# Second-block projections in products of 512 columns

## The chip, the cores and the metric

The kernel runs on one core of a Trainium2 chip. The metric is the device time of one execution in microseconds; the time given is the median of the runs.

## The reference, cut to what matters

Two transformer blocks follow one another on 512 tokens of width 1024 (fp32). The first is a hybrid mixer (differential attention and a convolution), cross-attention and a convolutional feed-forward. The second, in which the change lies, is this:

```
h = rms_norm(x);  proj = h @ w_in                     # 1024 -> 9232
sb_qkv, gdn_qkv, gdn_z, gdn_b, gdn_a, gate_sb, gate_gdn = split(proj)
o_sb  = stick_breaking_attention(q, k, v)             # 8 heads of 128
gq, gk, gv = silu(causal_depthwise_conv(gdn_qkv))     # kernel of 4
o_gdn = rms_norm(gated_delta_rule_chunked(l2(gq), l2(gk), gv, g, beta)) * silu(z)   # 8 heads of 128
x = x + (sigmoid(gate_sb) * (o_sb @ w_branch_sb) + sigmoid(gate_gdn) * (o_gdn @ w_branch_gdn)) @ w_out
x = x + peer_ffn(rms_norm(x))                         # product-key experts
```

## The kernel before, in words

Every matrix product of fp32 values is made of three: an operand is split into a high and a low part, and `mm3` (L198) adds high by high, low of the moving operand by high of the weights, and high by low, all into one bank of PSUM. A weight chunk of 128 x 2048 comes by two DMAs into the tiles `wraw` (three buffers), and `load_w` (L204) splits it: ScalarE copies the high part `wh`, VectorE subtracts for `wl` (L194, L195). The activations lie transposed as `yh` and `yl`: 8 tiles of 128 features by 512 tokens.

The second block (`block2`, L791) runs several strands at once. `gdn_in` (L1093) loops over eight heads h. For each it projects one chunk for query and key (`w_gqk`) and one for value and z (`w_gvz`) by `proj_tr` (L308), whose two banks are given by a rotation of tags (`ROT`, L33): p, gd and sz for head 0, p alone from head 1 on; p has two banks. The emptied banks go through a convolution and silu on ScalarE, VectorE and GpSimd (L1124 and L1127 read the bank), through transposes (L1134), and to DRAM. Then `head` of `gdn` (L935) works on one head: transposes of the key (L950), products of key and query (L969), an inversion of a triangular matrix in six levels (L988 on GpSimd, L996, L1007 and L1009 on TensorE, with L1021 and L1028 on ScalarE and L1025 on VectorE in between), a recurrence over four groups of tokens (L1058 to L1073), a norm (L1080 on GpSimd), a transpose (L1083), and a split (L1086, L1088), after which the head's output goes to DRAM (L1089, L1090). Its products go to the banks gd and gs. Most of its tiles have one buffer, so one head follows the other. After every second head come the projections of two heads of the attention (`prep`, by `proj_nat2`, L1305, where the weights are the moving operand, 256 columns) and the attention itself (`stick`, L1228).

When all heads are written, `tile_out` (L835) makes eight chunks of gates from Y (L815) and four chunks of the attention's branch from its output O (L823), with banks of tag p, emptied by L809 to L813 or L824. Then `load_o` (L828) reads the delta rule's output back from DRAM into a new `yh` and `yl`, heads 0 to 6 first and head 7 by itself, and `branch` (L1316) multiplies it with `w_bg`, by `proj_tr` with tag bank, features out, 512 columns a product.

The order on each engine's queue isn't that of the program. `TileContext(nc, schedule_with_timeline_sim=True)` (L1624) has a planner lay out the instructions when the program is built: by priority, which is the order of the program moved by `tc.high_priority`, and by the durations that the planner holds. The heads of the delta rule are moved ahead by 1500 places (L22, L1174) and those of the attention by 200; the projections and gates fill what is left. On the chip each engine follows its queue in that fixed order.

In `proj_tr`, `first` is set for both chunks of head 0, and `lazy` says that the tag is a function, as it is for all heads.

Of the kernel before, what the change touches and what calls it, by code (L numbers as in the profile page):

```python
# [182 lines left out]
class Prog:  # L183
# [124 lines left out]
    def proj_tr(s, Y, chunk, evac, ntok=512, tag="bank", first=False, eng="act"):  # L308

        W = s.load_w(chunk, 2048, eng)  # L310
        lazy = callable(tag)
        b = [s.bank(tag() if lazy else tag) for f in range(2)]
        if lazy or first:
            ft = [(f, n) for f in range(2) for n in range(0, 512, 256)]
            for f, n in sorted(ft, key=lambda x: x[1]) if first else ft:
                t = slice(n, n + 256)
                for k in range(8):
                    s.mm3(b[f][:, t], W(256 * k + 128 * f, 128), (Y[0][:, k, t], Y[1][:, k, t]), k == 0, k == 7)
                if n:
                    evac(f, b[f])  # L320
            return
        for k0 in (0, 4):
            for f in range(2):
                for k in range(k0, k0 + 4):
                    s.mm3(b[f][:, :ntok], W(256 * k + 128 * f, 128), (Y[0][:, k, :ntok], Y[1][:, k, :ntok]),
                          k == 0, k == 7)
        for f in range(2):
            evac(f, b[f][:, :ntok])
# [506 lines left out]
    def tile_out(s, Y, w, out, pool, evac):  # L835

        nc = s.nc
        W = s.load_w(w)
        o = pool.tile([128, 1024], F32, name="out")
        for u in range(2):  # L840
            b = s.bank("p")
            for t in (slice(0, 256), slice(256, 512)):
                for k in range(8):
                    s.mm3(b[:, t], W(256 * k + 128 * u, 128), (Y[0][:, k, t], Y[1][:, k, t]), k == 0, k == 7)
            evac(o[:, 512 * u:512 * u + 512], b)
        nc.sync.dma_start(out, o)

# [780 lines left out]
```

## Time and profile before

| | us |
|---|---|
| median of 3 runs | 3012.7 (3009.31 to 3016.61) |
| profiled execution, its own time | 3021.56 |
| span of the profiled execution | 3019.8 |
| mean granted clock of TensorE, share of full speed | 0.983 |

The span runs from the first to the last instruction of the core; the execution's own time has 1.8 us around it. Engines are PE (TensorE's products), PEld (its weight loads), DVE (VectorE), ACT (ScalarE), POOL (GpSimd) and SP (SyncE, which issues most DMAs). A row of the timeline gives the start of an instruction and its duration; TensorE's products overlap, so that the distance of two starts says more than a duration. In brackets stands how long the engine was idle before it, and what ended that. A tile is named without its buffer's number: `p<-yh,wh` is a product of `yh` and `wh` into a bank with tag p. In the stretches and groups, "busy" is the sum of durations, laid over one another where they overlap.

### The profile page before, as it was taken

The numbers are of one execution on the slowest core, as the hardware profiler recorded it, in microseconds if no ns is written. First come the engines' busy times: TensorE is split into PE (matmuls) and PEld (weight loads), VectorE is DVE, ScalarE is ACT, GpSimd is POOL, SyncE is SP. The second block draws the span as 40 slices with busy tenths as digits, with TensorE's granted clock in tenths as the row PEclk, the third lists the DMA queues.
The fourth block names the chain that finished last, engine by engine and source line by source line (L and its number), as shares of the span: only waits on it lengthen the run. The fifth ranks groups of instructions, "written<-read, shape, count | busy, mean of one in ns | idle before, by whom it ended". The sixth has DMA issues, their size and how long they took to land. (4 is left out here: it accounts for less than half of the span.)

```text
span 3019.8 us, 44411 instructions
## 1 busy us (share of the span) xinstructions
PE 2901.3 (96%) x17102; PEld 2602.8 (86%) x17103; DVE 2012.7 (67%) x3633; ACT 1340.5 (44%) x2383; POOL 607.4 (20%) x587
## 2 busy tenths in 40 slices
PE   8999999999899999999999799997999999999998
PEld 7877878888789999999988599997888889988977
DVE  5986445553566676765345997775667788787875
ACT  5244433332455565656423345554334344444432
POOL 3001010000455555452200000000111222222210
PEclk9999999999999999999999899998999999999999
DMA  5321132223345555454763134445788899988985
GB/s 194 98 71 63 57 98 98 97 92 98 109 143 161 150 159 161 137 168 141 228 228 127 53 107 143 169 175 180 244 301 307 297 323 337 334 328 299 332 279 198
DMA packets 200149, 549.62 MB, mean 182 GB/s; under 512 B 17360, under 2 KB 90704, under 8 KB 179072
## 3 DMA queue, kind: packets, MB, share of 16 engines
q1 hardware_dynamic: 149184, 358.34, 36.0%
q0 software_dynamic: 49600, 184.76, 17.5%
q10 hardware_dynamic: 1152, 3.67, 0.4%
q8 instruction: 134, 2.20, 0.3%
q14 instruction: 79, 0.65, 0.1%
HBM read 476.52 MB, written 70.19 MB: 181 GB/s over the span
## 5 line engine op out<-in xcount | busy, mean ns | idle before, releaser
L195 DVE TENSOR_TENSOR wl<-wraw,wh 128x1024 fp32r<-128x1024 f32 x474 | 590.3, 1246 | 305.3 <-ACT wh L194 303.4
L194 ACT ACTIVATE wh<-wraw 128x1024 fp32r<-128x1024 f32 (+1 forms) x495 | 520.8, 1054 | 581.6 <-PE bank L201 126.7
L1412 POOL DMA_INDIRECT r<-in_uv_dram,eg x128 | 175.6, 1372 | 1162.7 <-ACT eg L1486 945.9
L202 PE MATMUL A<-yh,wl 128*128 128x384 f32 x1024 | 346.3, 338 | 7.5 <-DVE wl L195 7.4
L200 PE MATMUL A<-yh,wh 128*128 128x384 f32 x1024 | 345.6, 338 | 3.9 <-ACT wh L194 3.3
L201 PE MATMUL A<-yl,wh 128*128 128x384 f32 x1024 | 344.6, 336 | 0.0
L200 PE MATMUL acc<-wh 128*128 128x512 f32 x768 | 304.1, 399 | 19.4 <-ACT wh L194 19.4
L201 PE MATMUL acc<-wl,wh 128*128 128x512 f32 x768 | 305.5, 398 | 0.9 <-DVE wl L195 0.9
L202 PE MATMUL acc<-wh,wl 128*128 128x512 f32 x768 | 292.6, 397 | 3.8 <-DVE wl L195 3.8
L1415 DVE SCALAR_TENSOR_TENSOR r<-r,hx 128x1024 f32<-128x1024 f32 x128 | 156.3, 1221 | 110.1 <-DMA r<-in_uv_dram,eg 108.7
L200 PE MATMUL p<-yh,wh 128*128 128x256 f32 x736 | 214.1, 291 | 7.0 <-DVE l L195 3.8
L202 PE MATMUL p<-yh,wl 128*128 128x256 f32 x736 | 215.7, 293 | 1.4 <-DVE wl L195 1.4
L201 PE MATMUL p<-yl,wh 128*128 128x256 f32 x736 | 213.4, 290 | 0.0
L202 PEld LDWEIGHTS A<-yh,wl 128*128 128x128 f32 x1024 | 192.9, 188 | 10.6 <-DVE wl L195 10.5
L200 PEld LDWEIGHTS A<-yh,wh 128*128 128x128 f32 x1024 | 193.2, 189 | 8.5 <-ACT wh L194 4.2
L201 PEld LDWEIGHTS A<-yl,wh 128*128 128x128 f32 x1024 | 193.1, 189 | 3.7
L200 PEld LDWEIGHTS acc<-wh 128*128 128x128 f32 x768 | 146.2, 190 | 51.0 <-ACT wh L194 20.8
L201 PE MATMUL bank<-yl,wh 128*128 128x512 f32 (+1 forms) x480 | 184.1, 384 | 0.3 <-DMA yl<-od 0.3
L202 PE MATMUL bank<-yh,wl 128*128 128x512 f32 (+1 forms) x480 | 183.5, 383 | 0.0
L200 PE MATMUL bank<-yh,wh 128*128 128x512 f32 (+1 forms) x480 | 182.8, 383 | 0.1
L202 PEld LDWEIGHTS acc<-wh,wl 128*128 128x128 f32 x768 | 145.2, 189 | 39.0 <-DVE wl L195 5.1
L201 PEld LDWEIGHTS acc<-wl,wh 128*128 128x128 f32 x768 | 146.4, 191 | 33.6 <-DVE wl L195 3.2
(576 smaller groups left out, 6914.8 us busy)
## 6 DMA issues: line engine op xcount, KB each, us to landing
wraw<-in_ut_dram SPq DMA_DIRECT2D x128, 512.0 KB, 4.7
wraw<-in_uv_dram SPq DMA_DIRECT2D x128, 512.0 KB, 6.2
Gd<-g SPq DMA_DIRECT2D x24, 1024.0 KB, 4.4
g<-Gd SPq DMA_DIRECT2D x128, 192.0 KB, 7.6
wraw<-in_w_up_dram SPq DMA_DIRECT2D x44, 512.0 KB, 3.7
wraw<-in_w_sb_dram SPq DMA_DIRECT2D x24, 512.0 KB, 4.3
wraw<-in_w_down_dram SPq DMA_DIRECT2D x22, 512.0 KB, 3.8
wraw<-in_w_out_dram SPq DMA_DIRECT2D x16, 512.0 KB, 3.8
```

The source lines that it names most:

```text
L194: r = nc.scalar.activation(h, src, AF.Copy)
L195: s.sub = (nc.gpsimd if eng == "pool" else nc.vector).tensor_tensor(l, src, h.bitcast(F32), ALU.subtract)
L200: nc.tensor.matmul(out, lhsT=L[0], rhs=R[0], start=start, stop=False)
L201: nc.tensor.matmul(out, lhsT=L[0], rhs=R[1], start=False, stop=False)
L202: nc.tensor.matmul(out, lhsT=L[1], rhs=R[0], start=False, stop=stop)
L1412: nc.gpsimd.indirect_dma_start(out=r, out_offset=None, in_=a["uv"], in_offset=bass.IndirectOffsetOnAxis(ap=eg[:, j:j + 1], axis=0))
L1415: nc.vector.scalar_tensor_tensor(r[:, :1024], r[:, :1024], 1.0, hx, op0=ALU.mult, op1=ALU.mult, accum_out=act[:, c])
```

## The change

In `proj_tr`, where the tag is a function and the chunk isn't of head 0, each of the two halves of features is made as one accumulation of 8 x 3 products over all 512 tokens and then emptied, in place of two accumulations over 256 tokens each. In `tile_out` the two accumulations of 256 tokens become one of 512. The two chunks of head 0 keep their halves of 256 tokens, and so does `proj_nat2`, which the diff doesn't touch.

```diff
--- before.py
+++ after.py
@@ -310,9 +310,15 @@
         W = s.load_w(chunk, 2048, eng)
         lazy = callable(tag)
         b = [s.bank(tag() if lazy else tag) for f in range(2)]
-        if lazy or first:
+        if lazy and not first:
+            for f in range(2):
+                for k in range(8):
+                    s.mm3(b[f], W(256 * k + 128 * f, 128), (Y[0][:, k], Y[1][:, k]), k == 0, k == 7)
+                evac(f, b[f])
+            return
+        if first:
             ft = [(f, n) for f in range(2) for n in range(0, 512, 256)]
-            for f, n in sorted(ft, key=lambda x: x[1]) if first else ft:
+            for f, n in sorted(ft, key=lambda x: x[1]):
                 t = slice(n, n + 256)
                 for k in range(8):
                     s.mm3(b[f][:, t], W(256 * k + 128 * f, 128), (Y[0][:, k, t], Y[1][:, k, t]), k == 0, k == 7)
@@ -839,9 +845,8 @@
         o = pool.tile([128, 1024], F32, name="out")
         for u in range(2):
             b = s.bank("p")
-            for t in (slice(0, 256), slice(256, 512)):
-                for k in range(8):
-                    s.mm3(b[:, t], W(256 * k + 128 * u, 128), (Y[0][:, k, t], Y[1][:, k, t]), k == 0, k == 7)
+            for k in range(8):
+                s.mm3(b, W(256 * k + 128 * u, 128), (Y[0][:, k], Y[1][:, k]), k == 0, k == 7)
             evac(o[:, 512 * u:512 * u + 512], b)
         nc.sync.dma_start(out, o)
```

## Rows read from the trace of the kernel before

**Rows 1.** The page: span, and busy time of the engines (share, number of instructions).
```profile
span 3019.8 us, 44411 instructions
PE 2901.3 (96%) x17102; PEld 2602.8 (86%) x17103; DVE 2012.7 (67%) x3633; ACT 1340.5 (44%) x2383; POOL 607.4 (20%) x587
```

**Rows 2.** Stretches: us, busy us and instructions of PE, PEld, DVE, ACT, POOL; clock; DMA.
```profile
860.00:1335.00 475.00, 463.94 (x3805) 452.37 (x3806) 310.39 (x534) 276.57 (x577) 262.79 (x301) 1.00 0.51 152
1335.00:1476.00 141.00, 140.20 (x1164) 138.35 (x1164) 76.15 (x129) 87.42 (x181) 46.83 (x56) 1.00 0.56 174
1476.00:1529.40 53.40, 53.40 (x455) 52.59 (x455) 18.59 (x28) 15.54 (x27) 7.21 (x8) 1.00 0.78 256
```

**Rows 3.** Waits of PE, 860 to 1529 us: total us, times, longest us.
```profile
PE p L200 <- DVE l L195: 3.8, 2, 3.0
PE p L200 <- DVE cv L1127: 2.4, 1, 2.4
...
PE p L200 <- DVE out L812: 0.8, 1, 0.8
...
PE sz L1283 <- DVE spl L195: 0.2, 1, 0.2
```

**Rows 4.** Groups of products, by form, whole span.
```profile
L202 PE MATMUL p<-yh,wl 128*128 128x256 f32 x736 | 215.7, 293 | 1.4 <-DVE wl L195 1.4
L201 PE MATMUL p<-wl,yh 128*128 128x256 f32 x384 | 112.8, 294 | 0.0
L200 PE MATMUL p<-o,wh 128*128 128x256 f32 x128 | 36.6, 286 | 0.0
```

**Rows 5.** Timeline of PE, 256 columns: start us, us, line, operation, operands.
```profile
1345.27 0.28 PE L201 MATMUL p<-yl,wh 128*128 128x256 f32 x1
...
1347.78 0.28 PE L201 MATMUL p<-yl,wh 128*128 128x256 f32 x1
...
1517.99 0.28 PE L200 MATMUL p<-o,wh 128*128 128x256 f32 x1
...
1521.88 0.28 PE L200 MATMUL p<-o,wh 128*128 128x256 f32 x1
```

**Rows 6.** Timeline of PE, 512 columns: Y moving, then the weights moving.
```profile
1540.65 0.39 PE L202 MATMUL bank<-yh,wl 128*128 128x512 f32 x1
...
1547.45 0.39 PE L202 MATMUL bank<-yh,wl 128*128 128x512 f32 x1
...
1600.03 0.39 PE L200 MATMUL bank<-wh,zh 128*128 128x512 f32 x1
...
1609.08 0.40 PE L200 MATMUL bank<-wh,zh 128*128 128x512 f32 x1
```

**Rows 7.** Timeline of PE: first transposes of the first and of the last head.
```profile
842.66 0.65 PE L950 MATMUL gd<-cf,in 128*128 128x128 f32 x4 [2.30 <-DMA in<-gq]
...
1418.46 0.60 PE L950 MATMUL gd<-cf,in 128*128 128x128 f32 x4
```

**Rows 8.** Timeline around one step of the chain, VectorE and PE.
```profile
1449.31 0.28 DVE L1025 TENSOR_TENSOR U<-U,gd 128x128 f32<-128x128 f32 x1
...
1450.76 0.38 PE L1007 MATMUL gd<-cf,U 128*128 128x128 f32 x2
```

**Rows 9.** Timeline of the last head's end, and of the next stage's first wait.
```profile
1518.14 1.43 POOL L1080 TENSOR_TENSOR on<-on,r 128x512 f32<-128x512 f32 x1
...
1521.99 0.60 PE L1083 MATMUL gs<-cf,on 128*128 128x128 f32 x4
...
1523.42 0.63 ACT L1086 ACTIVATE oh<-in 128x512 fp32r<-128x512 f32 x1 [4.59 <-DVE in L1084]
...
1529.27 0.28 PE L202 MATMUL p<-o,wl 128*128 128x256 f32 x1
...
1538.93 0.50 PE L201 MATMUL bank<-yl,wh 128*128 128x512 f32 x1 [0.29 <-DMA yl<-od]
```

**Rows 10.** Group of the weights' second split, 805 to 1530 us.
```profile
L195 DVE TENSOR_TENSOR wl<-wraw,wh 128x1024 fp32r<-128x1024 f32 x79 | 109.0, 1380 | 51.3 <-ACT wh L194 50.9
```

## The prediction

> **What bounds the kernel now.** I began with the page, for the whole: TensorE is counted busy for 96% of the span [rows 1]. Then I took the table of stretches over the second block, which is the only place that the diff touches. From 860 to 1529 us TensorE is busy in 463.9 of 475, 140.2 of 141 and 53.4 of 53.4 us at a granted clock of 1.00, while VectorE and ScalarE are busy for two thirds of it at most [rows 2]. A busy TensorE can still be stalled inside, so the list of waits comes next: in those 669 us it names twelve kinds of wait, from 3.8 us down to 0.2 us, which add up to 12.5 us [rows 3]. So this stretch is set by what TensorE is given, in the order in which it is given.
>
> That order is fixed when the program is built, and it mixes two things: the chain of the gated delta rule, one head after the other, in short products; and wide products that fill the rest. The heads start their first transposes between 842.66 and 1418.46 us, so every 82.3 us (seven gaps) [rows 7]. Does the chain set this pace, or the filler? The timeline around one step answers it: VectorE's result U is there at 1449.59 us, and the transpose that reads it begins at 1450.76 us [rows 8]. Those 1.17 us went into filler products that stand ahead of it on TensorE's queue. The last head shows the same: its normed output is ready at 1519.57 us, and its transposes begin at 1521.99 us [rows 9]. Here the chain waits for TensorE, not the other way round.
>
> **What is replaced, and its count.** By the code, chunks of heads 1 to 7 make 7 x 2 chunks x 2 halves of features x 2 x 24 = 1344 products of 256 columns; the function for gates and the first branch makes 12 chunks x 2 x 2 x 24 = 1152. The groups agree: 736 of each kind on yh and yl, and 128 on the attention's output [rows 4], of which 32 of each kind belong to the two first projections, which stay (the rest of those lies in other banks). The 384 of each kind with the weights moving stay too. So 2496 products become 1248 of 512 columns, 1056 of them on yh and yl and 192 on the attention's output. The number of columns stays, and so do the loads, the splits and the DMAs; 1248 weight loads go.
>
> **What a product costs.** The duration of one row, some 0.28 us, is no price: products overlap. The price is the distance between starts. From 1345.27 to 1347.78 us there are 21 products of 256 columns on yh and yl, 119.5 ns apart; on the attention's output 33 lie between 1517.99 and 1521.88 us, 117.9 ns apart [rows 5]. The next stage does what the change will do (features out, Y moving, 512 columns): 30 products from 1540.65 to 1547.45 us, 226.7 ns apart [rows 6]. With the weights moving, the same width takes 39 products in 9.05 us, 232.1 ns [rows 6]. I take 226.7, since there the same operand moves, and keep 232.1 as the other end. A pair then saves 2 x 119.5 - 226.7 = 12.3 ns on Y and 2 x 117.9 - 226.7 = 9.1 ns on the attention's output:
> 1056 x 12.3 + 192 x 9.1 = 13.0 + 1.7 = **14.7 us**. With 232.1 it is 1056 x 6.9 + 192 x 3.7 = 8.0 us.
>
> A rule speaks against this. The Trainium skill, "TensorE: Matmul & The Clock Gate", section "Back-to-back issue gap", gives a warm product its columns at 2.4 GHz and a fixed 2.5 ns; by that a pair would save 2.5 ns and the change 3.1 us. The rows don't agree: above their columns at that clock they leave about 13 ns, at either width.
>
> **What is given back.** First, the banks. A bank is filled by 24 x 226.7 = 5.4 us of products instead of 48 x 119.5 = 5.7 us, so whoever empties it has 0.3 us less before its turn comes again. Four waits of the list are of this kind, two on VectorE's l and one each on cv and out (7.0 us). I add 0.3 us to each, 1.2 us; if all 52 fillings came to wait it would be 15.6 us, but VectorE, busy 310 of 475 us, has room [rows 2]. The splits of weights (1.38 us each on VectorE, two a chunk [rows 10]) have 10.9 us a chunk instead of 11.5: nothing.
>
> Second, the seam with the next stage. The last head's output goes to DRAM and back, and the first product that needs it stands at 1538.93 us, 15.5 us after its split began at 1523.42 us [rows 9]. Two covers lie in between: the last 5.9 us of 256-column filler, to 1529.4 us, and 9.5 us of products of the next stage that don't need this head. Today they just do: the product waited 0.29 us [rows 9]. If head and filler shrink alike, the wait grows by 5.9 x 12.3 / 239 = 0.3 us. If the order puts the filler a little earlier against the chain, the first cover goes, 5.9 us. There is a reason for that: a step of the chain that comes ready while a product runs waits on average half a product, 113 instead of 60 ns, so the chain falls back against the filler. I take the upper end, **6.0 us**.
>
> Sum: 3012.7 - 14.7 + 1.2 + 6.0 = **3005 us** (3005.2). The profiled execution took 3021.6 us, 0.3% above the median of the runs; I take the difference from the median. Later stages are costed at nothing: they begin behind the norms, where TensorE waits for the whole residual, and their instructions are the same; I keep 2 us either way for an order that comes out differently there.
>
> **The rivals.**
> - *The whole saving stays.* The order keeps as many columns between two steps of the chain, and the seam costs 0.3 us. For it: the step above had 1.17 us to spare, and a step's share of the saving is about 0.1 us. Against it: the seam has no room today. 3012.7 - 14.7 = 2998 us.
> - *Nothing stays, because the chain keeps its pace.* If the planner that orders the queues holds the wide product for cheaper, it puts more columns between steps; the heads stay at 82.3 us, and the filler runs out earlier by what was saved. The 14.7 us then stand as idle TensorE before the last head ends, and only what the chain gains when it runs alone comes back: 3009 to 3013 us. For it: chain and filler end within 6 us of each other now. Against it: alone, a step has 1.2 us less to wait, so part must come back.
> - *Slower: the coarse products delay the chain.* Per head some 21 steps stand one behind the other on TensorE (the two pairs of tiles run side by side). Each waits half a product more, 54 ns: 21 x 0.054 x 8 = 9 us, and with the cover at the seam gone 15 us, while TensorE's saving is spent idle: up to 3028 us. It decides where a step has less to spare than this, so it needs a chain without slack; the 1.17 and 2.4 us above speak against it.
> - *No difference, because time goes by columns.* If what a product takes above its columns were hidden in this mixed order, a wide one would last as long as the two, 239 ns, and the time would stay at 3012.7 us. The page named above comes near this, with 3009.6 us. The rows at 226.7 ns speak against it.
>
> **How the numbers follow.** The forecast has 0.45, its own range 3001 to 3009 us; the whole saving 0.20; nothing 0.17; slower 0.15; by columns 0.03. A measurement of this kernel can tell 0.2%, 6.0 us, from no change. Faster than 3006.7 us: 0.36 of the forecast and nearly all of the whole saving, 0.55. Slower than 3018.7 us: 0.15. The rest, 0.30, lies between. The range of 2996 to 3016 us begins 2 us below the whole saving and takes in the end with 232.1 ns and the case with nothing left; outside stay most of the slower case and a few hundredths below.
>
> **What would show it.** Right: 512-column products on p about 227 ns apart, 1248 fewer of them; heads closer than 82.3 us, near 81; the first product of the next stage earlier than 1529.4 us by some 14 us; a wait of some 6 us for yl, the last head read back, early in that stage. Wrong: products at 239 ns; head starts still 82.3 us apart with TensorE idle in the last head; or waits of chain steps on TensorE turned into waits of TensorE for U, T or y.

## The result, and the profile after

The change made the kernel slower: 3053.98 us in the median (3040.89 to 3066.00, 6 runs) beside 3011.29 us of the kernel before on the same chip; the ratio is 1.0136, its 95% interval 1.0109 to 1.0164. The profiled execution took 3053.09 us. Each profile below is of one execution, and those of e1, e2 and e10 lie at the slow end of their kernel's runs, those of e4, e5 and e7 at the fast end, so idle time and clock read from a profile are that execution's.

The page of the profile after, which answers to [rows 1]:

```profile
span 3051.3 us, 41921 instructions
PE 2907.2 (95%) x15855; PEld 2545.5 (83%) x15855; DVE 2006.0 (66%) x3633; ACT 1341.4 (44%) x2383; POOL 607.1 (20%) x587
```

TensorE has 1247 products fewer (one record is missing of the 1248), and yet it is busy 6 us longer. Groups of products after, by form, for [rows 4]:

```profile
L202 PE MATMUL p<-yh,wl 128*128 128x512 f32 x352 | 143.2, 407 | 0.0
L200 PE MATMUL p<-o,wh 128*128 128x512 f32 x64 | 26.9, 423 | 7.3 <-DMA o<-od 7.3
L202 PE MATMUL p<-yh,wl 128*128 128x256 f32 x32 | 9.0, 283 | 0.0
```

So the change does what it says. The time is lost in one stretch, from the first head's first transposes to the first product of the next stage. Stretches of before (us; busy us and instructions of PE, PEld, DVE, ACT, POOL; clock; DMA): all eight heads, then the last.

```profile
842.70:1529.40 686.70, 673.58 (x5532) 658.67 (x5533) 415.34 (x703) 389.00 (x799) 328.66 (x375) 1.00 0.54 165
1418.50:1529.40 110.90, 110.90 (x932) 109.53 (x930) 47.17 (x73) 49.88 (x94) 29.52 (x33) 1.00 0.67 216
```

The same after: all eight heads, the seventh, the eighth, and the rest of the kernel.

```profile
845.30:1568.50 723.20, 681.85 (x4308) 603.18 (x4308) 410.67 (x702) 389.78 (x799) 324.78 (x372) 0.97 0.52 157
1416.40:1524.50 108.10, 100.61 (x511) 84.26 (x510) 40.83 (x67) 42.82 (x84) 21.44 (x28) 0.94 0.52 170
1524.50:1568.50 44.00, 32.87 (x221) 27.07 (x219) 14.16 (x34) 14.10 (x41) 20.01 (x24) 0.95 0.55 170
1568.50:3051.30 1482.80, 1419.82 (x7515) 1270.23 (x7513) 1096.43 (x2182) 620.54 (x1070) 186.57 (x138) 0.98 0.67 238
```

The stretch is 36.5 us longer. TensorE's idle time in it (length less busy) went from 13.12 to 41.35 us, 28.2 more. The clock's records in the trace have 42.1 us at the lower level, 1.2 GHz, where before had 6.8. In 9.3 of the 42.1 us TensorE was idle, which is counted already; it was busy in 32.7 us of them, and before in all 6.8. If half of what is busy at half clock is lost, that is 16.4 against 3.4 us, 13.0 more. What TensorE was busy for at full clock is then an estimate: 681.9 - 16.4 = 665.5 us against 673.6 - 3.4 = 670.2, so that 4.7 us of saving are left in this execution. 28.2 + 13.0 - 4.7 = 36.5. (Ahead of the stretch stand 24 of the 1248 products, behind it none. The part ahead took from 841.5 to 849.7 us in the profiles of this study, 842.7 in that of before; the part behind from 1475.6 to 1495.1 us, 1490.4 in that of before. I see no relation to the edits in either.)

Waits of TensorE in the stretch after, for [rows 3] (total us, times, longest us):

```profile
PE p L200 <- DMA o<-od: 7.3, 1, 7.3
PE p L200 <- ACT D L967: 5.1, 1, 5.1
PE gs L1088 <- POOL on L1085: 4.7, 1, 4.7
PE gd L1012 <- DVE U L1030: 3.8, 3, 2.5
PE sz L200 <- DMA qk<-sq: 3.6, 2, 3.4
PE gs L1063 <- ACT on L1078: 3.2, 5, 0.8
```

These aren't the waits of [rows 3] grown longer, but others: TensorE's queue now has something at its head that isn't ready. How the queue was laid anew shows when one counts, in the trace, the columns of filler (products of weights with Y or O) between the first transposes of one head and those of the next:

| head | before: us | columns | after: us | columns |
|---|---|---|---|---|
| 1 | 84.4 | 121,000 | 89.6 | 131,000 |
| 2 | 82.7 | 104,000 | 97.5 | 123,000 |
| 3 | 83.9 | 101,000 | 101.0 | 138,000 |
| 4 | 82.8 | 104,000 | 89.4 | 104,000 |
| 5 | 80.2 | 104,000 | 89.3 | 109,000 |
| 6 | 83.0 | 105,000 | 104.2 | 150,000 |
| 7 | 78.9 | 101,000 | 108.1 | 158,000 |
| 8 | 110.9 | 181,000 | 44.0 | 8,000 |

The planner laid more columns between the steps of the chain, the filler was used up when the last head began, and that head ran nearly alone. Timeline of after: the first transposes of the first and last head (for [rows 7]), the first and last of eighteen wide products on Y, the longest wait, and the last head's end (for [rows 9]); start, us, line, operands, in brackets the idle time ahead of it.

```profile
845.33 0.66 PE L955 MATMUL gd<-cf,in 128*128 128x128 f32 x4 [2.75 <-DMA in<-gq]
...
1391.56 0.39 PE L200 MATMUL p<-yh,wh 128*128 128x512 f32 x1
...
1395.44 0.39 PE L202 MATMUL p<-yh,wl 128*128 128x512 f32 x1
...
1460.80 1.00 PE L1001 MATMUL gd<-T,pm 128*128 128x64 f32 x8
1469.13 0.76 PE L200 MATMUL p<-o,wh 128*128 128x512 f32 x1 [7.34 <-DMA o<-od]
...
1474.78 0.63 PE L200 MATMUL p<-o,wh 128*128 128x512 f32 x1
1475.20 0.63 PE L201 MATMUL p<-o,wh 128*128 128x512 f32 x1
...
1524.50 0.60 PE L955 MATMUL gd<-cf,in 128*128 128x128 f32 x4
...
1567.70 1.11 PE L1088 MATMUL gs<-cf,on 128*128 128x128 f32 x4 [4.74 <-POOL on L1085]
1568.46 0.78 PE L200 MATMUL bank<-yh,wh 128*128 128x512 f32 x1
```

At 1469.13 us the first product of the attention's output chunk stands at the head of the queue and its operand isn't back from DRAM; the chain's steps stand behind it. Right after, products start 0.43 us apart: the clock is at its lower level (1465.0 to 1478.7 us in its records).

### The profile page after: what moved, and what is told of

The parts are those of the page before. It is cut to its first block, busy times and chain, and to the rows that moved or that the text cites. A ratio compares the mean times of both kernels' runs of the same rounds, so it can differ in the third digit from the quotient of the medians.

```text
span 3051.3 us, 41921 instructions
## 1 busy us (share of the span) xinstructions
PE 2907.2 (95%) x15855; PEld 2545.5 (83%) x15855; DVE 2006.0 (66%) x3633; ACT 1341.4 (44%) x2383; POOL 607.1 (20%) x587
## 5 line engine op out<-in xcount | busy, mean ns | idle before, releaser
L195 DVE TENSOR_TENSOR wl<-wraw,wh 128x1024 fp32r<-128x1024 f32 x474 | 581.9, 1228 | 293.9 <-ACT wh L194 291.4
L1424 DVE SCALAR_TENSOR_TENSOR x<-r,wt,x 128x1024 f32<-128x1024 f32 x128 | 163.7, 1279 | 12.8 <-ACT wt L1423 12.8
L200 PE MATMUL p<-yh,wh 128*128 128x512 f32 (+1 forms) x384 | 154.0, 401 | 9.4 <-ACT D L967 5.1
L1422 ACT ACTIVATE wt<-act 128x1 f32<-128x1 f32 x128 | 25.8, 202 | 301.8 <-DVE r L1420 301.8
```

What stands on the lines that cost most here:

```text
L195: s.sub = (nc.gpsimd if eng == "pool" else nc.vector).tensor_tensor(l, src, h.bitcast(F32), ALU.subtract)
L200: nc.tensor.matmul(out, lhsT=L[0], rhs=R[0], start=start, stop=False)
L1422: nc.scalar.activation(wt[:, c], act[:, c], AF.Gelu)
L1424: nc.vector.scalar_tensor_tensor(x, r[:, 1024:], wt[:, c], x, op0=ALU.mult, op1=ALU.add)
```

## The experiments

Three theories stood against each other. The order: the planner's queue for the wide products, not the products, costs the time. The product: a wide one costs more than its two halves in this mixed stretch. The tail: of the order, it is the last head without filler that counts.

### e1: wide products, TensorE's old queue

Added to the changed kernel, at the end of the program: one edge of order (no semaphore, no wait) from each product to the next, along a table of TensorE's queue in the kernel before, from the first place where the two queues differ to the last product changed.

```diff
+def in_order(tc):
+    every = [i for i in tc.nc.cur_bb.bb.instructions if type(i).__name__ == "InstMatmult"]
...
+    for x, y in zip(queue, queue[1:]):
+        tc.add_manual_dep(every[y], every[x].name,
+                          mybir.DependencyInfo(mybir.DependencyClass.NoSync, mybir.DependencyReason.DATA),
+                          reason="order")
```

> The changed kernel with every product of 512 columns, but TensorE's queue put by hand into the order of the kernel before (each wide product stands where the later of its two halves stood). If the order is the cause (theory: the planner lays too many columns between two steps of the chain, once they come as wide products, and the filler is used up before the last head), the loss is gone and what I forecast is seen: 2995 to 3008 us, heads 79 to 83 us apart, the first product of the next stage at 1515 to 1530 us. If the wide product itself is the cause (it costs more than two of 256 beside the rest), the time stays at 3040 to 3060 us.

Measured: 3017.04 us in the median, ratio 1.0005 (0.9995 to 1.0016). The loss is gone, and with it the product theory; but the gain that I had forecast isn't there either. Its stretch of the eight heads:

```profile
849.70:1535.50 685.80, 669.98 (x4308) 594.76 (x4309) 417.29 (x702) 388.11 (x799) 327.23 (x375) 0.99 0.54 165
```

Idle 15.8 us, and 17.1 us at the lower clock, all of them busy: 661.4 us busy at full clock, 8.7 less than before, given back by 2.7 us more idle time and 5.1 us more of halved clock.

### e2: narrow products, the changed kernel's queue

The same function in the kernel before, with the changed kernel's queue (two halves where a wide product stands).

> The opposite corner: every product of 256 columns as before, but TensorE's queue in the order of the changed kernel (two narrow products where a wide one stands). If the order is the cause: as slow as the changed kernel or slower by the 10 to 15 us that the wide products save, 3050 to 3075 us, with the last head of 40 to 50 us almost without filler. If the wide product itself is the cause: 3005 to 3020 us, as before.

Measured: 3086.58 us, ratio 1.0233 (1.0208 to 1.0257): the queue alone costs more than the whole change, and more than I had expected from it (3050 to 3075 us). The eight heads and the last of them:

```profile
844.90:1603.80 758.90, 712.35 (x5532) 689.35 (x5532) 409.01 (x703) 394.83 (x799) 326.55 (x373) 0.94 0.49 150
1548.60:1603.80 55.20, 45.95 (x237) 39.97 (x235) 13.62 (x34) 14.61 (x41) 20.13 (x24) 0.64 0.43 136
```

TensorE idles 46.6 us, and in the last head of this execution it ran at a granted clock of 0.64. With e1 and the two kernels this makes a square: in the old queue the width is worth nothing that can be told (1.0000 to 1.0005), in the new one it wins (1.0233 to 1.0136); the queue costs at either width (1.0005 to 1.0136, and 1.0000 to 1.0233).

### e3 and e4: one half of the change each, the planner free

```diff
-            for t in (slice(0, 256), slice(256, 512)):
-                for k in range(8):
-                    s.mm3(b[:, t], W(256 * k + 128 * u, 128), (Y[0][:, k, t], Y[1][:, k, t]), k == 0, k == 7)
+            for k in range(8):
+                s.mm3(b, W(256 * k + 128 * u, 128), (Y[0][:, k], Y[1][:, k]), k == 0, k == 7)
```

This hunk alone is e3; the other alone is e4. (The columns in the expectations are those of the queue and hold the attention's own products too.)

> Only the gates and the attention's output chunks as wide products (24 of the 52 places), the chunks of q, k, v and z by halves as before. In the planner's queue the first six heads keep the columns they had before; the seventh gets 186,000 and the last 110,000 (before 112,000 and 185,000). By the order theory the last head still has filler for its whole chain, so the time is 3003 to 3015 us. If every wide product costs something of its own, 24/52 of the loss: about 3031 us.

> Only the chunks of q, k, v and z as wide products (28 of the 52 places), gates and output chunks by halves as before. In the planner's queue the first three heads get 132,000, 136,000 and 148,000 columns, the other five 107,000 to 120,000, the last 107,000. By the order theory no head runs out of filler: 3000 to 3015 us, with the first three heads longer and the last shorter than before. If every wide product costs something of its own, 28/52 of the loss: about 3034 us.

Measured: e3 3026.11 us, ratio 1.0036 (1.0022 to 1.0050); e4 3052.70 us, ratio 1.0134 (1.0114 to 1.0155). Both expectations failed. e4 loses as much as the whole change, though its last head has 108,000 columns of filler in the trace: a last head without filler can't be the whole of it. The stretches of e4 (heads 1 to 5, heads 6 to 8) and the last head of e3:

```profile
843.60:1308.00 464.40, 447.78 (x2992) 404.64 (x2993) 307.18 (x513) 271.62 (x552) 249.69 (x277) 0.98 0.50 148
1308.00:1555.20 247.20, 234.43 (x1894) 228.19 (x1892) 105.28 (x190) 118.62 (x247) 80.26 (x96) 0.96 0.58 181
```

```profile
1447.20:1544.40 97.20, 84.88 (x422) 71.22 (x420) 30.24 (x51) 27.12 (x57) 26.00 (x28) 0.86 0.60 197
```

In e4 TensorE idles 16.6 us in the first five heads and 12.8 in the last three, and 40.3 us run at the lower clock; in e3 the last head has 12.3 us idle at a clock of 0.86. The loss is spread, as idle time and as halved clock.

### e5, e6, e7 and e11: the old order on all engines

e1 had held TensorE's queue alone, and the planner had laid the other four anew. Here all five are held, through the whole kernel: e5 with all products wide, e6 with those of `tile_out`, e7 with the chunks, and e11 as e5, but with a wide product in the place of the earlier half in place of the later. Against e1:

```diff
-    every = [i for i in tc.nc.cur_bb.bb.instructions if type(i).__name__ == "InstMatmult"]
+    for name, runs in (x.split("=") for x in zlib.decompress(base64.b85decode(ORDER)).decode().split(";")):
+        every = [i for i in tc.nc.cur_bb.bb.instructions
+                 if str(i.engine) == "EngineType." + name and type(i).__name__ != "BassTilePoolBoundary"]
```

> Every wide product, and now the queues of all five engines (TensorE, VectorE, ScalarE, GpSimd, SyncE) held in the order of the kernel before, through the whole kernel. In e1 only TensorE's queue was held, and the stretch of the eight heads took 685.8 us against 686.7: busy time without the halved clock fell by some 8.7 us, idle time rose by 2.7 and the halved clock cost 5.1 more. If that give-back comes from the other engines' changed order, it goes, and the time is 3002 to 3009 us. If it lies in the wide products themselves (TensorE comes sooner to points that wait for the same transfers), the time stays within 0.2% of before: 3009 to 3018 us.

> Only the gates and the attention's output chunks wide (24 places, 576 wide products), all queues in the order of the kernel before. By the order theory the loss of e3 (12 us) goes altogether and 576 x 5 to 7 ns, some 3 to 4 us, are won: 3008 to 3013 us. If the wide products of this part cost something of their own: 3020 to 3030 us, as e3.

> Only the chunks of q, k, v and z wide (28 places, 672 wide products), all queues in the order of the kernel before. By the order theory the loss of e4 (39 us) goes and 672 x 8 ns, some 5 us, are won, less what waits give back: 3006 to 3016 us. If the wide products of this part cost something of their own: 3040 to 3055 us, as e4.

> As e5 (all products wide, all queues in the order of the kernel before), but each wide product stands where the earlier of its two halves stood. If e5's gain of 9 us is the wide products' own, it is seen again: 3003 to 3010 us. If it hung on that one placement, the time is within 0.2% of before: 3010 to 3020 us.

Measured, as ratios to before: e5 0.9977 (0.9962 to 0.9992), 3006.08 us; e6 0.9985 (0.9973 to 0.9997); e7 0.9989 (0.9977 to 1.0001); e11 0.9971 (0.9958 to 0.9984). All lie where the order theory has them, though the interval of e7 takes in 1.0000, no change. e5 and e11 beat both kernels; against the one before by 0.23% and 0.29%, some 7 and 9 us. Stretches of e5 (all heads, last head):

```profile
844.90:1518.20 673.30, 662.94 (x4307) 589.87 (x4308) 415.90 (x702) 386.90 (x799) 327.04 (x374) 1.00 0.55 168
1409.30:1518.20 108.90, 108.90 (x576) 91.17 (x575) 47.62 (x73) 49.20 (x95) 29.64 (x32) 1.00 0.68 220
```

Idle 10.4 us (13.1 before), 3.4 us at the lower clock (6.8), in 2.8 of them busy, so 661.54 us busy at full clock, 8.6 less than the 670.17 before. The heads start 80.6 us apart (844.86 to 1409.31 us, seven gaps) where they started 82.3. And the attention's output and the seam, in e5's timeline:

```profile
1505.18 0.39 PE L202 MATMUL p<-o,wl 128*128 128x512 f32 x1
...
1510.68 0.39 PE L202 MATMUL p<-o,wl 128*128 128x512 f32 x1
1510.91 0.60 PE L1088 MATMUL gs<-cf,on 128*128 128x128 f32 x4
...
1518.00 0.39 PE L202 MATMUL p<-o,wl 128*128 128x512 f32 x1
1518.23 0.39 PE L200 MATMUL bank<-yh,wh 128*128 128x512 f32 x1
...
1528.45 0.50 PE L201 MATMUL bank<-yl,wh 128*128 128x512 f32 x1 [0.97 <-DMA yl<-od]
```

The first wait for the last head's output is 0.97 us where it was 0.29 [rows 9]. Between the last head's transposes and the next stage lie 7.3 us of filler (1510.91 to 1518.23 us), where before had 7.4 (1521.99 to 1529.38). The waits for a bank that the prediction priced, in e5:

```profile
PE p L200 <- DVE l L195: 1.4, 2, 0.7
...
PE p L200 <- DVE cv L1132: 1.1, 1, 1.1
...
PE p L200 <- DVE out L818: 0.7, 1, 0.7
```

They add up to 3.2 us, where the same three were 7.0 [rows 3].

### e8 and e9: repairs that leave the planner free

e8 holds gates and output chunks back behind the first transposes of a later head:

```diff
                 for f in range(8):
-                    s.tile_out(Y, s.a["w_gate"][f], s.gd[f], to, gate)
+                    with tc.issue_after(s.start[5 if f < 3 else 6 if f < 7 else 7]):
+                        s.tile_out(Y, s.a["w_gate"][f], s.gd[f], to, gate)
...
-                        s.tile_out(O, s.a["w_bs"][c], s.yd[c], to,
-                                   lambda o, b: nc.vector.tensor_tensor(o, b, next(gs), ALU.mult))
+                        with tc.issue_after(s.start[7]):
+                            s.tile_out(O, s.a["w_bs"][c], s.yd[c], to,
+                                       lambda o, b: nc.vector.tensor_tensor(o, b, next(gs), ALU.mult))
```

> The changed kernel with a hold on TensorE's queue alone: gates 0 to 2 not ahead of the sixth head, 3 to 6 not ahead of the seventh, gate 7 and the output chunks not ahead of the eighth. The last three heads get 104,000, 104,000 and 121,000 columns in the planner's queue instead of 162,000, 162,000 and 7,000; the first five are as in the changed kernel. If the last head without filler is the main loss (about 30 us of idle TensorE), most of it returns: 3020 to 3035 us. If the loss is spread over all heads as waits and halved clock (in e4 the last head kept 107,000 columns and the time was as bad): 3040 to 3058 us.

e9 holds the beginning of each of the 75 banks of filler (first product, count, step of the chain):

```diff
+HOLDS = (
+    (4100, 24, 3970), (4128, 24, 3974), (4156, 24, 3976), (4285, 48, 3982), (4337, 48, 3998), (4389, 48, 4006),
...
+    for first, n, step in HOLDS:
+        for i in every[first:first + n]:
+            tc.add_manual_dep(i, every[step].name,
+                              mybir.DependencyInfo(mybir.DependencyClass.NoSync, mybir.DependencyReason.DATA),
+                              reason="hold")
```

> The changed kernel with 75 holds on TensorE's queue and nothing else: no bank of filler products begins ahead of the step of the chain behind which it begins in the kernel before (within a bank, and on the other engines, the planner orders as it likes). The heads get 124,000, 116,000, 110,000, 110,000, 119,000, 105,000, 116,000 and 179,000 columns in the planner's queue, near to those of before. If the number of columns between two steps is what matters, and not the exact order, most of the loss goes: 3005 to 3022 us. If it takes the exact order of the old queue: 3025 to 3055 us.

Measured: e8 3034.71 us, ratio 1.0063 (1.0043 to 1.0082); e9 3038.41 us, ratio 1.0082 (1.0068 to 1.0096). So with filler put back into the last head about half of the loss was gone, and the other half stays. In e9 each head has 98,000 to 123,000 columns and the last 177,000, as before, and still some 25 us are lost: how many columns a head gets isn't what decides alone. It may be which product stands between which two steps, or the order of the other four engines, which the planner laid anew here; e9 doesn't part the two. Stretch and first waits of e9:

```profile
843.50:1555.80 712.30, 679.04 (x4308) 599.30 (x4309) 423.30 (x702) 385.36 (x799) 328.79 (x374) 0.98 0.53 158
```

```profile
PE gd L1012 <- DVE U L1030: 6.3, 5, 2.2
PE gd L1012 <- POOL U L1019: 4.2, 3, 3.1
PE gd L1001 <- ACT y L1026: 3.5, 6, 1.1
PE gd L1001 <- ACT T L1033: 3.4, 4, 1.7
```

The waits of the kernel before for the same steps, in its stretch:

```profile
PE gd L1007 <- POOL U L1014: 0.9, 1, 0.9
PE gd L1007 <- DVE U L1025: 0.8, 1, 0.8
```

TensorE idles 33.3 us in e9, and the first four waits are for the chain's own steps: a step stands at the head of the queue before its operand is there.

### e10: spare products in two waits

All queues held in the changed kernel's own order, and products that nobody reads put into the two long waits of the timeline above:

```diff
+            d = s.bank("so")
+            s.spare = [[nc.tensor.matmul(d[:, :256], lhsT=Y[0][:, 0, :128], rhs=Y[0][:, 0, :256], start=True, stop=True).ins
+                        for i in range(n)] for n in (58, 38)]
```

> The changed kernel in its own order, all queues held, with 96 spare products of 256 columns into a bank that nobody reads: 58 (some 7 us) behind the product at 1461.5 us of the changed kernel's trace, where TensorE waits 7.6 us for the attention's output, and 38 (some 4.6 us) behind the one at 1562.7 us, where it waits 5.0 us for the last head's norm. Nothing is waited for less. If the idle time brings the halved clock that stands behind both waits (1465.0 to 1478.7 and 1564.0 to 1570.8 us, 20.5 us together), the clock stays full there and 8 to 10 us are won against the changed kernel: ratio to before 1.010 to 1.011, 3041 to 3046 us. If the clock falls for another reason, the time is the changed kernel's, 1.0136, 3050 to 3058 us.

Measured: 3068.31 us, ratio 1.0176 (1.0161 to 1.0190): by the medians slower than the change by itself, which neither reading had expected. The profiled execution took 3082.42 us. The stretches of the seventh and eighth head:

```profile
1411.00:1516.00 105.00, 103.66 (x569) 87.91 (x568) 40.46 (x66) 42.95 (x84) 21.58 (x28) 1.00 0.54 175
1516.00:1585.50 69.50, 54.63 (x258) 48.16 (x257) 15.23 (x35) 14.85 (x42) 20.12 (x24) 0.64 0.31 99
```

The first half went as the idle reading has it: with the wait filled the seventh head kept a clock of 1.00 (0.94 after) and took 105.0 us in place of 108.1. In the eighth the clock fell at 1525.1 us and stayed low for 34.1 us, though the longest wait ahead of that was 1.5 us:

```profile
1524.21 0.44 PE L1015 MATMUL gd<-cf,U 128*128 128x128 f32 x2 [1.53 <-POOL U L1022]
1525.38 0.80 PE L1066 MATMUL gs<-S,kc 128*128 128x128 f32 x2 [0.73 <-ACT on L1081]
```

In the changed kernel the same instructions ran at full clock but for the last 4.5 us. So where the wait was filled the clock stayed up, but in a head without filler it fell all the same, without a long wait ahead of it. What decides that is left open.

The end of the eighth head shows a cost that the spare products made themselves:

```profile
1568.60 0.37 ACT L1081 ACTIVATE on<-gs,rq 128x128 f32<-128x128 f32 x1 [2.49 <-PE gs L1073]
...
1577.00 0.95 POOL L842 DMA_DIRECT2D yh<-od  x1 [29.06 <-issue]
...
1578.91 1.06 POOL L1083 TENSOR_TENSOR sq<-on 128x512 f32<-128x512 f32 x1
...
1583.19 1.12 PE L1091 MATMUL gs<-cf,on 128*128 128x128 f32 x4 [8.14 <-POOL on L1088]
```

They read Y, whose buffer the load of the next `yh` takes over. Its issue on GpSimd was held until the last of them was done, at 1575.05 us, and it went out at 1577.00 us (in the changed kernel at 1550.73 us). Behind it in that queue stands the head's norm: it began 9.9 us after its operand was there (1568.97 to 1578.91 us), in the changed kernel 0.1 us after. From the end of the chain to the next stage e10 took 16.5 us, the changed kernel 5.1. So 11.4 of the 25.5 us by which this head is longer come from where the spare products read, and what filling the second wait would win is not shown. The other 14.1 us lie in the chain, which ran at the lower clock in 40.5 of its 53.0 us (1516.0 to 1568.97 us).

### e12: narrow products, another plan

```diff
-FILL = [1, 3, 5, 7]
+FILL = [2, 4, 6, 7]
```

> The kernel before, every product of 256 columns, but the four pairs of attention heads traced behind heads 2, 4, 6 and 7 in place of 1, 3, 5 and 7, so that the planner has to lay the whole stretch anew: 125,000, 113,000, 113,000, 112,000, 102,000, 115,000, 113,000 and 186,000 columns for the eight heads. If it is the wide products that the planner lays badly, a new plan of narrow ones is about as good as the old: 3008 to 3025 us. If the old order is a lucky one, and any new plan costs 20 to 40 us as those of the kernels with wide products did: 3030 to 3055 us.

Measured: 3023.60 us, ratio 1.0023 (1.0008 to 1.0037). Its own eight heads took 687.9 us, 16.8 us of them idle. This new plan of narrow products costs 0.2%; that of wide ones, the changed kernel against e5, 1.6% (1.0136 and 0.9977). So not every new plan costs what the wide ones' did. Yet it is one other plan, with nearly the old columns a head (96,000 to 126,000, the last 183,000), and no more were tried: that the planner fits wide products worse than narrow ones in general is not shown.

## Why the prediction was wrong, and where it was right

**The step that failed** is the one on what is given back: there I costed a new order at the seam alone, with 6.0 us, and summed everything else as if each queue stayed as it was, with narrower distances. That the planner would lay the queue by its own durations stood in my text, as a rival, but its price had a wrong bound: I let TensorE idle for no more than the 14.7 us saved. The new queue moved tens of thousands of columns from the last head into the third, sixth and seventh, and put TensorE in front of operands that weren't there. It cost 28.2 us of idle time and 13.0 us of halved clock. That it was the queue is shown by e1, e2 and e5. Why this order fits the chip so much worse than the old one is not shown; that the planner holds a wide product for too cheap is my reading of the table of columns, no more. Another reading was left untested: the heads are moved ahead by 1500 places of the program's order, and a place that holds a wide product is worth twice the columns, so the same constant reaches over more filler than it did.

**The saving** was right in kind and too large in size. The term that was too large is that of a pair. The distance of two wide products that I took as 226.7 ns is 228 in the changed kernel where eighteen follow each other undisturbed (1391.56 to 1395.44 us, 17 distances) and 229 on the attention's output in e5 (1505.18 to 1510.68 us, 24 distances), and over the whole stretch of e5 the median of those on Y at full clock is 231, beside 120 of the narrow ones before. The whole came to 8.6 us in e5 and 8.7 in e1 in place of 14.7, near my low end of 8.0. By the rule that the Trainium skill, "TensorE: Matmul & The Clock Gate", section "Back-to-back issue gap", gives for a single product's gap, it would have been 3.1 us; the runs don't agree with that either, for 8.6 us over the 1224 pairs of the stretch are 7.0 ns a pair, not 2.5.

**The banks** (1.2 us) and **the seam** (6.0 us): in the old order neither came. The bank waits of the list fell from 7.0 to 3.2 us in e5, all idle time by 2.7 us, and the wait for yl grew by 0.7 us: head and filler shrank alike, which I had worked out at 0.3 us and set aside. My reason for the upper end, that a step waits half a product more and the chain falls back against the filler, isn't seen: the filler behind the last head's transposes is 7.3 us where it was 7.4, and the heads of e5 are closer together, not further apart. With that the mechanism of my slower rival falls too. Its side was right; its end at 3028 us wasn't.

**What bounds the kernel** was right for the queue that I read: with all queues held, some 8.6 us less of work made the kernel 7 us faster in e5 and 9 us in e11. Both readings by which I had called the chain the one that waits [rows 8, rows 9] are from the last head, which has 181,000 columns of filler where the others have 101,000 to 121,000; that the first seven follow TensorE too is shown only by e5, where they come 80.6 us apart. What bounds one queue need not bound another, and the change made another. Of my signs, the 1248 products and nearly their spacing came as said, the others not; of the signs against, the last head with TensorE idle and the waits of TensorE for U and T came, with heads not 82.3 but 97 us apart (845.33 to 1524.50 us, seven gaps).

## What to carry to other kernels

Where a planner lays the queues when the kernel is built, a change of an instruction's width is two changes, the instruction and the whole order, and the second was about five times the first here. Price the two apart: hold the old order on every engine by edges and measure the instruction alone (here 0.9977), and look at what the new order puts between the steps of the chain before trusting it. To hold a part was not enough: one engine's queue alone (1.0005) or the beginnings of the banks (1.0082) gave the gain away. And look at what a probe itself holds up: the spare products of e10 read a tile whose buffer a later load was waiting for.

## What the runs showed of the hardware

Idle time and halved clock came together here: 28.2 us more of the one with 13.0 us more of the other, and after the wait of 7.34 us wide products started 0.43 us apart instead of 0.23. That the wait brought the clock down is borne out by the seventh head of e10 alone, where the wait was filled and the clock stayed at 1.00. In a last head without filler the clock went either way for nearly the same instructions, 0.95 in the changed kernel and 0.64 in e2 and e10, each in one profile.

The wide product starts 228 to 231 ns after the one ahead of it in this stretch and 226.7 in the next stage [rows 6]; I found nothing in the traces that explains the few ns.
